# The 31 dependent steps of a block inverse issued on POOL in place of DVE

## The chip, the cores and the metric

The kernel runs on one core of a Trainium2 chip. The metric is the device time of one launch in microseconds (us), the median of several runs. One execution was also taken by the profiler; every row below comes from it. PE is the tensor engine, DVE the vector engine, ACT the scalar engine, POOL the GpSimd engine, and SP the engine whose queue issues the DMAs.

## The reference

Two transformer blocks run one after the other on one sequence of 1024 tokens of width 1024. The first has a projection, a sliding-window attention, an RWKV-7 time mix, an output projection and a convolution-gated feed-forward network. The second has gated linear attentions and a stick-breaking attention. Only the RWKV part is touched:

```python
def step(state, inp):
    r_t, w_t, k_t, v_t, kk_t, a_t = inp
    sa = jnp.einsum('bhvk,bhk->bhv', state, -kk_t)
    state = (state * w_t[:, :, None, :]
             + sa[..., None] * (kk_t * a_t)[:, :, None, :]
             + v_t[..., None] * k_t[:, :, None, :])
    return state, jnp.einsum('bhvk,bhk->bhv', state, r_t)
...
_, o = lax.scan(step, state0, (tmaj(rh), tmaj(heads(decay)), tmaj(kh), tmaj(vh), tmaj(kk), tmaj(heads(a))))
```

There are 8 heads of width 64. A token's state update depends on the state that the token before it left. The kernel takes the tokens in chunks of 64, and inside a chunk the dependence becomes the inverse of a triangular 64 x 64 matrix.

## The kernel before

The sequence is cut into two halves of 512 tokens, and each half into four pieces of 128 tokens. The RWKV part of one piece is numbered e (0 to 7) and has three stages. `rwkv_a(e)` makes the operands and the triangular matrices (tile `MT`); it uses POOL for two products of 128 x 512 (`kk`, `r`) and for one power (`rn`, line 127). `rwkv_b(e)` inverts the matrices. `rwkv_c(e)` runs over the two chunks of the piece with the state and normalises the result; its power on POOL is `rsd`.

In `rwkv_b` the 32 diagonal blocks of 32 x 32 of one piece go through DRAM (`l_d`) into the tile `Lq`, one block on each partition and four copies of all of them. The inverse `XT` is then built by forward substitution in 31 steps. A step is one product into `ot` (line 544) and one sum into `XT` (line 545), so there are 62 instructions a piece and 496 in all, each dependent on the one before it. Between steps the stage yields, and other work is written in between. The result goes by DMA to `x_d` (line 548) and from there into `TT` (line 550); DVE transposes `TT` into `XQ` (line 553), and PE takes `XQ` in the products of line 558 and goes on to the whole 64 x 64 inverse.

All products with weights are made of three passes, with high and low parts of both factors. The helper `split` (line 130) makes the parts: ACT copies to `wh`, and DVE subtracts to `wl`. Weights come in through tiles with three buffers (`wr`, `wh`, `wl`), loaded by line 137 from SP's queue.

The order of the work is made in two steps, both before anything runs. `weave` takes the stages of several streams in turn by the costs that they yield (0.7 for one step of the inverse) times a rate for each stream. A planner then gives each engine's queue and SP's queue one fixed order, by priorities, by what depends on what, and by when it takes a thing to be ready. `Stream` raises the priority of the RWKV stages by a number of places (`AA`, `AB`, `AC`). Nothing is reordered at run time: each queue is worked off in order, and an instruction whose input is late holds up all that stands behind it in its queue. The streams of the first four pieces are woven with the projection; those of the last four with the output projection and the feed-forward network:

```python
weave(Stream(proj_all(), RF), Stream(stage_a(), R1, AA), Stream(stage_b(), R2, AB), Stream(stage_c(), R3, AC), also=[attend])
...
def rest():
    for e in range(4, 8):
        yield from rwkv_a(e, 1)
        yield from rwkv_b(e, 1)
        yield from rwkv_c(e, 1)
```

Elementwise operations go through the helper `tt` (line 80), whose last argument is the engine. `V` is DVE and `G` is POOL. `PE0` and `PE1` (line 90) name the engines of even and odd steps, and both are `V`.

Of the kernel before, what the change touches and what calls it, by code (L numbers as in the profile page):

```python
# [65 lines left out]
def tile_hybrid_blocks(ctx: ExitStack, tc: tile.TileContext, a: dict, out: bass.AP):  # L66
    nc = tc.nc
    V, S, G, T, SY = nc.vector, nc.scalar, nc.gpsimd, nc.tensor, nc.sync
# [7 lines left out]
    def act(out, in_, func, **kw):  # L76
        S.activation(out=out, in_=in_, func=func, **kw)  # L77

    def tt(out, in0, in1, op, eng=None):
        (eng or V).tensor_tensor(out=out, in0=in0, in1=in1, op=op)  # L80
# [6 lines left out]
        (eng or V).tensor_scalar(out=out, in0=in0, scalar1=s1, scalar2=s2, op0=op0, **kw)  # L87

    DQ = SY
    PE0, PE1 = V, V  # L90
    ADD, SUB, MUL, MAX, MIN = ALU.add, ALU.subtract, ALU.mult, ALU.max, ALU.min

    cst = pool("cst", 1)
# [296 lines left out]
    def after(what):  # L390
        while what not in done1:
            yield None
# [7 lines left out]
    def flat(t):  # L400
        return t.rearrange("p a b -> p (a b)")
# [125 lines left out]
    def rwkv_b(e, dbl):  # L527
        yield from after(("a", e))
        z, AR, MT, UV, BKt, EC, bon, l_d, x_d = rws[e]
        psr_t = psb_r  # L530


        Lq = rw.tile([128, 32, 32], F32, tag="Lq" if dbl == 2 else "t4", name="Lq", bufs=1)
        for g in range(4):
            DQ.dma_start(out=Lq[32 * g:32 * g + 32], in_=l_d)
        XT = rw.tile([128, 8, 32], F32, name="XT")
        G.memset(XT, 0.0)
        for g in range(4):
            G.memset(flat(XT[32 * g:32 * g + 32])[:, g:256:36], 1.0)
        ot = rw.tile([128, 80], F32, name="ot")  # L540
        for s in range(31):
            n, m = s // 4 + 1, 31 - s
            o3 = ot[:, 0:n * m].rearrange("p (a b) -> p a b", a=n)
            tt(o3, Lq[:, s:s + 1, s + 1:32].to_broadcast([128, n, m]), XT[:, 0:n, s:s + 1].to_broadcast([128, n, m]), MUL, PE1 if s % 2 else PE0)
            tt(XT[:, 0:n, s + 1:32], XT[:, 0:n, s + 1:32], o3, ADD, PE1 if s % 2 else PE0)
            yield 0.7
        for g in range(4):
            DQ.dma_start(out=x_d.rearrange("q (a g) t -> g q a t", g=4)[g], in_=XT[32 * g:32 * g + 32])
        for b in range(2):
            DQ.dma_start(out=TT[32 * b:32 * b + 32, :, 32 * b:32 * b + 32], in_=x_d[16 * b:16 * b + 16].rearrange("q s t -> s q t"))  # L550

        XQ = rw.tile([64, 16, 32], F32, name="XQ")
        V.transpose(out=XQ[0:32], in_=TT[0:32, :, 0:32])
        qp = psr_t([128, 8, 32])
        for n in range(8):
            for b in range(2):
                q = 8 * b + n
                T.matmul(out=qp[32 + 64 * b:64 + 64 * b, n, :], lhsT=MT[0:32, q // 2, q % 2, 96:128], rhs=XQ[0:32, q, :],
                         start=True, stop=True)
        for b in range(2):  # L560
            act(XQ[32:64, 8 * b:8 * b + 8], qp[32 + 64 * b:64 + 64 * b], AF.Copy)
        yield 4
        qp = psr_t([128, 8, 32])
        for n in range(8):
            for b in range(2):
                q = 8 * b + n
                T.matmul(out=qp[64 * b:64 * b + 32, n, :], lhsT=XQ[32:64, q, :], rhs=TT[32:64, q, 32:64], start=True, stop=True)
        for b in range(2):
            act(TT[0:32, 8 * b:8 * b + 8, 32:64], qp[64 * b:64 * b + 32], AF.Copy)
        yield 3  # L570


        ap_ = psr_t([128, 8, 64])
        for q in range(16):
            hb = 64 * (q % 2)
            T.matmul(out=ap_[hb:hb + 64, q // 2, :], lhsT=UV[0:64, q // 2, hb:hb + 64], rhs=TT[:, q, :], start=True, stop=True)
        act(AR[:, :, 1, :], ap_, AF.Copy)
        yield 3

        wp_ = psr_t([128, 8, 64])  # L580
        for n in range(8):
            for b in range(2):
                q = 8 * b + n
                hb = 64 * (q % 2)
                T.matmul(out=wp_[64 * b:64 * b + 64, n, :], lhsT=MT[64:128, q // 2, q % 2, 64:128], rhs=UV[64:128, q // 2, hb:hb + 64],
                         start=True, stop=True)
        W0 = []
        for b in range(2):
            W0.append(rw.tile([64, 8, 64], F32, tag="W0" if dbl == 2 else "t3", name="W0", bufs=2))
            V.tensor_copy(W0[b], wp_[64 * b:64 * b + 64])  # L590
        yield 4
        yp = psr_t([128, 8, 64])
        for n in range(8):
            for b in range(2):
                T.matmul(out=yp[64 * b:64 * b + 64, n, :], lhsT=TT[:, 8 * b + n, :], rhs=W0[b][:, n, :], start=True, stop=True)
        for b in range(2):
            act(flat(UV[0:64, 4 * b:4 * b + 4, :]), flat(yp[64 * b:64 * b + 64]), AF.Copy)
        yield 4
        done1.add(("b", e))
# [224 lines left out]
    def stage_b():  # L824
        for e in range(4):
            yield from rwkv_b(e, 2)
# [12 lines left out]
# [5 lines that stand above are left out]
# [888 lines left out]
```

## Time and profile before

| what | value |
|---|---|
| median of 3 runs | 2511.98 us (2508.98 to 2515.89) |
| the profiled execution, its own time | 2509.05 us |
| span from its first to its last instruction | 2507.3 us |
| mean granted clock of PE over the span | 0.981 |

The profiled execution's own time is 1.75 us more than its span, and 2.9 us less than the median of the runs. A busy share is the time in which an engine had an instruction in work. The granted clock is the share of PE's full speed (2.4 GHz) that the chip allowed; it has two levels, full and half, so a mean of 0.9 over a stretch is a fifth of it at half speed. In rows with an arrow and a releaser, the number in brackets is how long the engine had been idle, and behind `<-` stands what ended that.

### The profile page before, as it was taken

Reading aid. Unit: us, or ns where it says so; the run is one execution under the profiler, and the core shown is the slowest. Engines: PE = TensorE matmul, PEld = TensorE weight load, DVE = VectorE, ACT = ScalarE, POOL = GpSimd, SP = SyncE. Lnnn points to the kernel's source line nnn. Section 1 sums busy time; section 2 is a strip of 40 time slices with the busy share of each in tenths; the row PEclk is TensorE's granted clock in tenths of the full one; section 3 lists DMA queues with packets and bytes.
Section 4 is the critical chain, followed back from the end, with each engine's and each line's share of the span. In section 5 each row is a group of like instructions: output and inputs, shape, how many; then the busy total and the mean of one; then the engine's idle time right before and its main releaser. Section 6 shows DMA issues by size and latency. Waiting matters only on the chain.

```text
span 2507.3 us, 40921 instructions
## 1 busy us (share of the span) xinstructions
PE 2375.0 (95%) x15310; PEld 1863.7 (74%) x15310; DVE 1688.9 (67%) x3678; ACT 1171.0 (47%) x2223; POOL 100.2 (4%) x138
## 2 busy tenths in 40 slices
PE   6989998889999999999999999999999999999997
PEld 5767776767777777778778887788877667777665
DVE  5466556667686776663885555555568988788887
ACT  4345433654433434343543333343345575656863
POOL 1001000100000000000000000000000000000000
PEclk9999999979999999999999999999999999999989
DMA  6433323555352342333463332243256335342446
GB/s 203 147 116 89 99 87 94 160 162 159 97 172 79 107 140 91 92 124 96 161 205 94 97 93 93 81 156 100 94 166 223 99 112 179 105 132 91 144 136 244
DMA packets 219997, 320.77 MB, mean 128 GB/s; under 512 B 56956, under 2 KB 95508, under 8 KB 219799
## 3 DMA queue, kind: packets, MB, share of 16 engines
q1 hardware_dynamic: 219798, 318.17, 40.5%
q8 instruction: 120, 1.97, 0.3%
q14 instruction: 79, 0.64, 0.1%
HBM read 270.88 MB, written 47.21 MB: 127 GB/s over the span
## 4 chain that ended last, share of the span: by engine, by line
PE 60%; DVE 9%; DMA 3%; issue 3%; ACT 2%; POOL 1%; SPq 0%; POOLq 0%; ACTq 0%; DVEq 0%
PE g L153 32%; PE d L153 12%; DVE wl L80 1%; PE s L1416 1%; PE R L1520 1%; PE gr L773 1%; DVE cv L83 1%; PE gr L774 1%; PE gr L775 1%; PE x L773 1%; PE x L775 1%; PE x L774 1%; DVE tmp L80 1%; PE z L1505 1%; PE po L1538 1%
## 5 line engine op out<-in xcount | busy, mean ns | idle before, releaser
L77 ACT ACTIVATE wh<-wr 128x512 fp32r<-128x512 f32 x712 | 442.8, 626 | 639.8 <-PE g L153 216.9
L153 PE MATMUL g<-hi,wl 128*128 128x512 f32 (+1 forms) x1680 | 677.1, 403 | 13.5 <-DVE lo L80 4.1
L153 PE MATMUL g<-hi,wh 128*128 128x512 f32 (+1 forms) x1680 | 667.2, 397 | 0.0
L153 PE MATMUL g<-lo,wh 128*128 128x512 f32 (+1 forms) x1680 | 665.5, 396 | 0.0
L80 DVE TENSOR_TENSOR wl<-wr,wh 128x512 fp32r<-128x512 f32 x712 | 484.7, 685 | 207.2 <-ACT wh L77 205.9
L153 PEld LDWEIGHTS g<-hi,wl 128*128 128x128 f32 (+1 forms) x1680 | 317.1, 189 | 91.0 <-issue 8.6
L153 PEld LDWEIGHTS g<-hi,wh 128*128 128x128 f32 (+1 forms) x1680 | 316.7, 188 | 71.7 <-issue 2.6
L153 PEld LDWEIGHTS g<-lo,wh 128*128 128x128 f32 (+1 forms) x1680 | 317.2, 189 | 68.5 <-issue 3.7
L83 DVE SCALAR_TENSOR_TENSOR cv<-g,CW,cv 128x511 f32<-128x511 f32 (+1 forms) x256 | 190.8, 745 | 179.3 <-ACT cv L77 179.0
L153 PE MATMUL d<-hh,wl 128*128 128x512 f32 x512 | 202.5, 399 | 12.7 <-ACT hh L77 7.5
L153 PE MATMUL d<-hl,wh 128*128 128x512 f32 x512 | 202.1, 395 | 0.1
L153 PE MATMUL d<-hh,wh 128*128 128x512 f32 x512 | 200.8, 392 | 0.0
L77 ACT ACTIVATE cv<-g,CW 128x512 f32<-128x512 f32 x128 | 99.5, 777 | 181.5 <-PE g L153 181.1
L80 DVE TENSOR_TENSOR acc<-d,acc 128x512 f32<-128x512 f32 x112 | 76.4, 689 | 94.7 <-PE d L153 94.6
L153 PEld LDWEIGHTS d<-hh,wl 128*128 128x128 f32 x512 | 95.8, 189 | 41.8 <-ACT hh L77 12.0
L153 PEld LDWEIGHTS d<-hl,wh 128*128 128x128 f32 x512 | 96.5, 188 | 23.0 <-DVE hl L80 3.6
L153 PEld LDWEIGHTS d<-hh,wh 128*128 128x128 f32 x512 | 96.6, 189 | 20.3 <-issue 0.2
L773 PE MATMUL gr<-wl,hi 128*128 128x512 f32 x200 | 83.4, 418 | 7.3 <-DVE wl L80 6.6
L774 PE MATMUL gr<-wh,lo 128*128 128x512 f32 x200 | 80.1, 400 | 0.0
L775 PE MATMUL gr<-wh,hi 128*128 128x512 f32 x200 | 79.7, 399 | 0.0
L127 POOL TENSOR_TENSOR rs<-ms,half_c 128x1 f32<-128x1 f32 x48 | 29.4, 612 | 1085.1 <-DVE ms L87 1077.2
L77 ACT ACTIVATE hh<-cv 128x512 fp32r<-128x512 f32 x64 | 40.4, 631 | 65.5 <-DVE cv L80 65.4
(508 smaller groups left out, 3475.7 us busy)
## 6 DMA issues: line engine op xcount, KB each, us to landing
wr<-in_w_up_dram SPq DMA_DIRECT2D x256, 256.0 KB, 2.7
wr<-in_w_in_dram SPq DMA_DIRECT2D x160, 256.0 KB, 2.9
wr<-in_w_down_dram SPq DMA_DIRECT2D x128, 256.0 KB, 2.6
wr<-in_w_out_dram SPq DMA_DIRECT2D x100, 256.0 KB, 3.0
wr<-in_w_values_dram SPq DMA_DIRECT2D x64, 256.0 KB, 2.9
wa<-in_w_ada_dram SPq DMA_DIRECT2D x24, 512.0 KB, 4.3
xt<-x SPq DMA_DIRECT2D x24, 512.0 KB, 4.5
xt<-in_x_dram SPq DMA_DIRECT2D x16, 512.0 KB, 3.6
```

The source lines that it names most:

```text
L77: S.activation(out=out, in_=in_, func=func, **kw)
L80: (eng or V).tensor_tensor(out=out, in0=in0, in1=in1, op=op)
L83: V.scalar_tensor_tensor(out=out, in0=in0, scalar=scalar, in1=in1, op0=op0, op1=op1)
L127: G.tensor_tensor(out=dst, in0=src, in1=half_c[0:src.shape[0], 0:src.shape[1]], op=ALU.pow)
L153: T.matmul(out=ps, lhsT=l, rhs=r, start=(first and n == 0), stop=(last and n == 3 * len(wk) - 1))
L773: T.matmul(out=p, lhsT=hi[:, k, tok], rhs=wl, start=first, stop=False)
L774: T.matmul(out=p, lhsT=lo[:, k, tok], rhs=wh, start=False, stop=False)
L775: T.matmul(out=p, lhsT=hi[:, k, tok], rhs=wh, start=False, stop=last)
L1416: T.matmul(out=ps[hb:hb + 64, l - 2, :], lhsT=xl(hb, l, 0, 64), rhs=xl(hb, l, 0, 64), start=True, stop=True)
L1505: T.matmul(out=z[:, h, :], lhsT=Ks[:, p, h, kb * 128:(kb + 1) * 128], rhs=q[:, h, off:], start=q is ql, stop=q is qh)
L1520: T.matmul(out=R[:, :, c0:c1], lhsT=m, rhs=x[:, :, c0 - off:c1 - off], start=start and x is sl, stop=x is sh, skip_group_check=not start)
L1538: T.matmul(out=po[hb:hb + 64, c0:c1], lhsT=Vh[:, kb, hd * 64:(hd + 1) * 64], rhs=ar[:, h, c0 - off:c1 - off], start=(kb == top), stop=(kb ...
```

## The change

Both instructions of each of the 31 steps are issued on POOL. The names `PE0` and `PE1` are dropped. Nothing else in the text of the kernel differs; the two fills of `XT` (lines 537 and 539) were on POOL already.

```diff
     DQ = SY
-    PE0, PE1 = V, V
     ADD, SUB, MUL, MAX, MIN = ALU.add, ALU.subtract, ALU.mult, ALU.max, ALU.min
...
         for s in range(31):
             n, m = s // 4 + 1, 31 - s
             o3 = ot[:, 0:n * m].rearrange("p (a b) -> p a b", a=n)
-            tt(o3, Lq[:, s:s + 1, s + 1:32].to_broadcast([128, n, m]), XT[:, 0:n, s:s + 1].to_broadcast([128, n, m]), MUL, PE1 if s % 2 else PE0)
-            tt(XT[:, 0:n, s + 1:32], XT[:, 0:n, s + 1:32], o3, ADD, PE1 if s % 2 else PE0)
+            tt(o3, Lq[:, s:s + 1, s + 1:32].to_broadcast([128, n, m]), XT[:, 0:n, s:s + 1].to_broadcast([128, n, m]), MUL, G)
+            tt(XT[:, 0:n, s + 1:32], XT[:, 0:n, s + 1:32], o3, ADD, G)
             yield 0.7
```

## Rows read from the trace of the kernel before

**Rows 1.** The page: engines, busy us (share of the span), instructions.

```profile
PE 2375.0 (95%) x15310; PEld 1863.7 (74%) x15310; DVE 1688.9 (67%) x3678; ACT 1171.0 (47%) x2223; POOL 100.2 (4%) x138
```

**Rows 2.** Windows cut at each chain's first and last step: busy us, granted clock.

```profile
core 0: us, PE busy (x) PEld busy (x) DVE busy (x) ACT busy (x) POOL busy (x), PEclk, DMA share, GB/s
157.00:186.70 29.70, 25.14 (x127) 18.97 (x126) 26.25 (x105) 12.22 (x24) 0.00 (x0) 0.90 0.47 150
...
307.30:340.20 32.90, 29.47 (x152) 23.16 (x153) 27.00 (x108) 15.79 (x41) 2.68 (x2) 0.90 0.18 57
...
516.60:554.90 38.30, 32.16 (x156) 25.32 (x155) 31.10 (x109) 21.65 (x49) 2.06 (x3) 0.82 0.46 143
...
1011.30:1040.70 29.40, 27.58 (x112) 21.63 (x111) 25.93 (x90) 9.95 (x16) 0.00 (x0) 0.94 0.27 81
sum 258.40, PE 235.04 PEld 184.11 DVE 226.34 ACT 100.40 POOL 9.57; mean PE 29.38 PEld 23.01 DVE 28.29 ACT 12.55 POOL 1.20
```

**Rows 3.** Sum over windows of the seven stretches between the chains, same columns.

```profile
sum 625.00, PE 597.59 PEld 474.12 DVE 374.32 ACT 282.02 POOL 38.47; mean PE 85.37 PEld 67.73 DVE 53.47 ACT 40.29 POOL 5.50
```

**Rows 4.** Waits of PE, 100 to 1060 us: for what, us, times, longest.

```profile
PE trx L247 <- DVE y L83: 6.3, 2, 5.9
```

**Rows 5.** The tile ot: duration ns min/median/max, first and last start us.

```profile
L80 DVE TENSOR_TENSOR ot<-Lq,XT x248: 164/211/727, 157.0 to 1040.3; 128x60 f32<-128x60 f32 x12, 128x54 f32<-128x54 f32 x8, 128x66 f32<-128x66 f32 x8, 128x28 f32<-128x28 f32 x8
```

**Rows 6.** POOL's groups by form: busy us, mean ns, idle before.

```profile
L127 POOL TENSOR_TENSOR rs<-ms,half_c 128x1 f32<-128x1 f32 x48 | 29.4, 612 | 1085.1 <-DVE ms L87 1077.2 <-DVE XT L80 7.9
L127 POOL TENSOR_TENSOR rn<-n,half_c 128x8 f32<-128x8 f32 x8 | 14.7, 1840 | 43.2 <-DVE n L87 43.2
...
L80 POOL TENSOR_TENSOR kk<-k,P 128x512 f32<-128x512 f32 x8 | 8.4, 1046 | 85.6 <-DMA k<-rkv_d 75.5 <-PE ra L495 10.1
...
L539 POOL MEMSET XT<- 32x8 f32 x32 | 3.4, 105 | 1.8
```

**Rows 7.** Timeline of POOL, then of DVE, 225 to 236 us: start, us.

```profile
227.46 1.05 POOL L80 TENSOR_TENSOR kk<-k,P 128x512 f32<-128x512 f32 x1
234.37 1.55 POOL L80 TENSOR_TENSOR r<-r,P 128x512 f32<-128x512 f32 x1 [5.86 <-DVE AR L80]
...
227.54 1.52 DVE L80 TENSOR_TENSOR og<-og,rsd 128x512 f32<-128x512 f32 x1 [1.82 <-POOL rsd L127]
...
234.34 0.68 DVE L80 TENSOR_TENSOR o<-o,bon 128x512 f32<-128x512 f32 x1
```

**Rows 8.** DVE's groups in the windows 379.9 to 401.7 and 699.8 to 736.8.

```profile
L80 DVE TENSOR_TENSOR wl<-wr,wh 128x512 fp32r<-128x512 f32 x6 | 4.1, 685 | 0.0
...
L80 DVE TENSOR_TENSOR wl<-wr,wh 128x512 fp32r<-128x512 f32 x12 | 8.2, 686 | 0.5 <-ACT wh L77 0.5
L83 DVE SCALAR_TENSOR_TENSOR adam<-wa,sc,adam 128x1024 f32<-128x1024 f32 x5 | 6.4, 1281 | 0.5 <-DMA wa<-in_w_ada_dram 0.5
```

**Rows 9.** The chain of piece 3 in the timelines of SP, DVE and PE.

```profile
369.65 2.49 SPq L535 DMA_DIRECT2D Lq<-l_d  x4
379.88 0.18 DVE L80 TENSOR_TENSOR ot<-Lq,XT 128x31 f32<-128x31 f32 x1
401.76 2.53 SPq L548 DMA_DIRECT2D x_d<-XT  x4
404.40 1.47 SPq L137 DMA_DIRECT2D wr<-in_w_out_dram  x2
406.08 0.87 SPq L550 DMA_DIRECT2D TT<-x_d  x2
409.38 0.70 DVE L553 STREAM_TRANSPOSE XQ<-TT 32x512 f32<-32x512 f32 x1 [0.53 <-DMA TT<-x_d]
410.13 0.69 PE L558 MATMUL rb__3723<-XQ,MT 32*32 32x32 f32 x32 [0.41 <-DVE XQ L553]
```

**Rows 10.** Waits of DVE over the span: for what, us, times, longest.

```profile
DVE sgw L462 <- POOL rn L127: 12.6, 8, 1.8
DVE XQ L553 <- DMA TT<-x_d: 1.3, 3, 0.5
```

## The prediction

> **What bounds the kernel now.** I read the page first. PE is busy for 95% of the span, and POOL for 4% [rows 1]. So the change takes work from the second busiest engine and gives it to an idle one, and it can help only where PE stands because of DVE. The windows tell how much that is. Cut at the first and the last step of each of the eight chains, they hold 258.4 us, in which PE is busy for 235.0 and DVE for 226.3 [rows 2]: DVE is 88% busy there and PE idle for 23.4 us (9.1%). The seven stretches between the chains hold 625.0 us, with DVE busy for 374.3 (60%) and PE idle for 27.4 us (4.4%) [rows 3]. PE stands about twice as much while a chain runs. The granted clock is also below 1 in four of the eight chain stretches (0.90, 0.90, 0.82, 0.94) [rows 2]; by their lengths that is 0.10 x 29.7 + 0.10 x 32.9 + 0.18 x 38.3 + 0.06 x 29.4 = 14.9 us of PE's full speed. Not all of it belongs to the chain: in the stretch with 0.82, PE stands once for 5.9 us for `y`, which is the normalisation after the output projection [rows 4].
>
> Then I followed one chain through the queues. For piece 3, SP issues the loads of `Lq` until about 372, the first step starts on DVE at 379.88, the last step ends at 401.7, `x_d` is issued at 401.76, `TT` at 406.08, DVE turns it into `XQ` at 409.38 after 0.53 us of waiting for it, and PE takes that at 410.13 after 0.41 us of waiting [rows 9]. The reader is to see how tight these places are. Over all eight pieces DVE stood for `TT` only three times, 1.3 us in all [rows 10]: the fixed order has the users of the chain just where the chain ends.
>
> **What goes from DVE.** 496 instructions of 0.211 us median [rows 5] are 105 us of busy time, 13 us a chain. Off the path this is worth nothing; on it, what counts is PE's idle time. If the chain stretches came down to the idle share of the others, 0.044 x 258.4 = 11.3 us would be left of 23.4, a gain of 12.1; with all the lost clock back it would be 27.0. The lower end is 0, as DVE still has its other work in one file. I take 10: most of the 12.1, hardly any of the clock, since its largest part hangs on `y` [rows 4].
>
> **What a step costs on POOL.** The trace has no small product or sum there. A step works on 31 to 80 elements a partition, on the mean 50.3 (the sum of n x m over the 31 steps is 1560). POOL's product of 512 elements takes 1.046 us and its fill of 8 elements 0.105 us [rows 6]. With the fill's time as the fixed part, the product is 0.105 + 1.84 ns an element, so an instruction takes 0.105 + 0.093 = 0.20 us, and 62 of them 12.3 us. The upper end comes from the powers: 0.612 us for one element and 1.840 for eight make 0.44 us fixed [rows 6]; the product then has 1.18 ns an element, an instruction takes 0.50 us, and 62 take 31 us. I take 0.33, a little nearer the product and the fill, which have no power in them: 20.5 us a chain.
>
> **What the two engines do to each other.** At 227.46 POOL begins `kk`, 1.05 us; at 227.54 DVE begins `og<-og,rsd`, and it takes 1.52 us instead of the 0.69 of its passes of that size; at 234.37 POOL's `r`, just behind the start of DVE's `o<-o,bon`, takes 1.55 instead of 1.05 [rows 6 to 8]. Each waits until the other's pass is over. The Trainium skill, SBUF — State Buffer, section "Who interferes with whom", has this as a rule: a DVE instruction with two SBUF inputs and a GpSimd instruction that reads SBUF exclude each other for the whole instruction; the trace agrees (1.52 against 0.69). By that rule the weight splits count and the passes that read PSUM do not. So DVE's passes with two SBUF inputs lie on top of the chain: in one chain stretch the splits alone are 4.1 us, in another the splits and `adam` are 8.2 + 6.4 = 14.6 [rows 8]. A chain of 20.5 us in place of a stretch of 258.4 / 8 = 32.3 us meets 0.63 of that, 2.6 to 9.3 us, in the middle 6. The chain is then about 26 us; it can start when `Lq` has landed, which is before DVE took it up [rows 9], so by the clock it should end no later than now.
>
> **Where that puts the stall.** The end by the clock is not what decides, but the end against the places in the order, which is made anew before the run. Three queues are in file behind the chain: SP at `x_d`, with weight loads behind it; DVE at `XQ`, with the next splits behind it; PE at line 558, with the next products behind it [rows 9]. The trace shows how the order treats POOL: the user of the power `rn` stands right behind it each time, and DVE stood for it 8 times of 8, 12.6 us in all [rows 10], 1.6 of the 1.84 us that the power takes [rows 6]. So the order has had POOL's results too early, by nearly their whole time. If it has the steps at their bare time and nothing for the mutual waits, `x_d`, `XQ` and line 558 come some 6 us too early a chain. While DVE stands, POOL works undisturbed, so I take a third off: 4 us of PE's time a chain. PE at 95% cannot make it up: 8 x 4 = 32 us. Below, this is 0, when the order has room; above, 62 x (0.50 - 0.33) = 10.5 us come on top of 6, 16 a chain, 130 us in all. The fills, the DMAs and their number do not change. The powers and products of the neighbouring pieces now share POOL with the steps; I cost them at nothing beyond this, as no more than three of them fall into the four stretches shown [rows 2].
>
> **The sum.** 2509.05 - 10 + 32 = 2531 us, for an execution like the profiled one, which is 2.9 us under the median of the runs.
>
> **The rivals.**
> - *The chain fits its places, and DVE's relief is what is left.* This is the other side. For it: POOL is free for 96% of the span [rows 1], and `Lq` is there some 4 us before DVE starts on it: the last load is issued about 8 us ahead, and a transfer with its issue takes about 4, as from `x_d` to `TT` [rows 9]. Against it: `rn`. The time is 2509 - 10 = 2499, down to 2490 if part of the clock comes back. It decides when a chain is less than 10 / 8 = 1.25 us late against its places.
> - *Nothing to measure.* Relief and stalls cancel, or PE stood for other things all along: 2509, within 0.3%. That bound, 7.5 us, is about what a measurement of this kernel can tell from no change. For it: only 23.4 of 2507 us are in play. It needs a chain late by 0.3 to 2.2 us.
> - *POOL is slow at small work.* With 0.50 us a step, the chain is 31 + 6 us, longer than DVE's 32.3, and 12 us late a chain after a fourth is taken off: 2509 - 10 + 96 = 2595. For it: the powers' fixed 0.44 us. Against it: the fill of 0.105 [rows 6]. The Trainium skill, GPSIMD Engine Reference, section 3.1, gives about 2.6 cycles an element at 1.2 GHz for two inputs and calls DVE about twice as fast; an estimate from that page is 50.3 x 2.6 / 1.2 = 109 ns of elements a step. The rows give 59 to 93 ns, and what a step costs beside them the page leaves open.
>
> **How the numbers follow.** The forecast has a chance of 0.43, slow small steps 0.07, the fitting chain 0.28, nothing to measure 0.22. So: slower 0.50, same 0.22, faster 0.28. The likeliest is slower, 2531; its own range is 2520 to 2572, from 2.6 to 9 us late a chain. The range over all cases is 2494 to 2572: it leaves out the best part of the fitting chain below, and slow steps above, together about 0.17.
>
> **What the profile after would show.** Steps right: 496 instructions of about 0.33 us on POOL, start to start, longer where DVE's two-input passes lie; DVE's busy time down by about 105 us; DVE's `XQ` and PE's line 558 waiting for `TT` in most pieces, about 4 us each, and SP standing at `x_d`. Wrong: if `XQ` still waits for no more than 1.3 us in all, the order had room, and the time is at or below that of before. The prediction would also be wrong if the new order moves the work of other pieces, so that the gaps of PE come from something that the chain doesn't touch.

## The result, and the profile after

The changed kernel takes 2636.32 us (median; 2623.52 to 2641.21), against 2510.48 us (2506.85 to 2515.89) for the kernel before on the same chip: a ratio of 1.0498, 95% interval 1.0472 to 1.0523. It is slower, as forecast, but by 126 us and not by 22, and outside the stated range of 2494 to 2572. The profiled execution has a span of 2632.7 us and a mean granted clock of 0.946. Lines of the changed kernel carry numbers one lower than before: `XQ` is line 552 and PE's product 557.

The page's line of engines (busy us, share, instructions):

```profile
PE 2437.0 (93%) x15310; PEld 1909.4 (73%) x15310; DVE 1615.4 (61%) x3182; ACT 1171.1 (44%) x2223; POOL 274.0 (10%) x634
```

Against [rows 1], PE's busy time is up by 62.0 us with the same 15310 matmuls, and its idle time (span less busy) went from 132.3 to 195.7 us, up by 63.4. The sum, 125.4, is the whole difference of the two spans. So half of the loss is PE standing, and half is PE doing the same work slower. The granted clock fits that: a mean of 0.946 over 2632.7 us is 2 x 0.054 x 2632.7 = 284 us at the lower level of 1.2 GHz, against 95 us for 0.981 over 2507.3.

Next the windows cut at each chain's first and last step, first, second and last chain and the sum (columns as in [rows 2]), and the sum over the seven stretches between them:

```profile
151.00:178.10 27.10, 20.44 (x96) 15.53 (x96) 12.63 (x21) 9.52 (x18) 22.31 (x63) 0.89 0.25 79
224.10:254.70 30.60, 20.36 (x94) 15.43 (x94) 17.87 (x43) 9.63 (x20) 25.98 (x65) 0.83 0.22 65
...
1122.10:1147.80 25.70, 21.12 (x89) 16.14 (x87) 13.64 (x24) 8.11 (x14) 20.89 (x62) 1.00 0.14 41
sum 219.70, PE 172.28 PEld 129.96 DVE 109.70 ACT 67.13 POOL 181.69; mean PE 21.53 PEld 16.25 DVE 13.71 ACT 8.39 POOL 22.71
```

```profile
178.10:224.10 46.00, 38.81 (x395) 32.27 (x396) 16.10 (x47) 14.57 (x44) 3.34 (x7) 0.62 0.29 78
...
339.00:384.50 45.50, 39.57 (x292) 28.45 (x291) 9.68 (x18) 10.22 (x25) 0.79 (x7) 0.55 0.30 85
...
sum 777.10, PE 715.03 PEld 567.69 DVE 414.29 ACT 313.78 POOL 40.14; mean PE 102.15 PEld 81.10 DVE 59.18 ACT 44.83 POOL 5.73
```

The chains are shorter than before (219.7 us against 258.4), and DVE is half idle in them (109.7 of 219.7). But PE stands for 47.4 us in them instead of 23.4, and for 62.1 between them instead of 27.4 [rows 2, 3]. The granted clock of 0.62 and 0.55 lies in the stretches behind the first and the third chain.

The steps themselves, by the tile `ot`:

```profile
L80 POOL TENSOR_TENSOR ot<-Lq,XT x248: 208/296/1102, 151.0 to 1147.3; 128x60 f32<-128x60 f32 x12, 128x54 f32<-128x54 f32 x8, 128x66 f32<-128x66 f32 x8, 128x28 f32<-128x28 f32 x8
```

A stretch of POOL's and of DVE's timeline in the chain of piece 1 (start, us, idle before):

```profile
238.51 0.30 POOL L80 TENSOR_TENSOR ot<-Lq,XT 128x64 f32<-128x64 f32 x1
238.89 0.32 POOL L80 TENSOR_TENSOR XT<-XT,ot 128x64 f32<-128x64 f32 x1
...
241.90 1.64 POOL L126 TENSOR_TENSOR rn<-n,half_c 128x8 f32<-128x8 f32 x1
...
247.00 0.81 POOL L80 TENSOR_TENSOR ot<-Lq,XT 128x48 f32<-128x48 f32 x1
247.89 0.29 POOL L80 TENSOR_TENSOR XT<-XT,ot 128x48 f32<-128x48 f32 x1
...
254.51 0.21 POOL L80 TENSOR_TENSOR XT<-XT,ot 128x8 f32<-128x8 f32 x1
```

```profile
234.51 0.17 DVE L87 TENSOR_SCALAR n<-ra 128x8 f32<-128x8 f32 x1 [0.33 <-PE ra L456]
...
243.58 0.52 DVE L461 COPY sgw<-rn 128x512 f32<-128x512 f32 x1 [8.56 <-POOL rn L126]
...
246.99 0.69 DVE L80 TENSOR_TENSOR kk<-kk,ia 128x512 f32<-128x512 f32 x1
```

An instruction of a step with 64 elements takes 0.30 to 0.32 us, and the next starts 0.38 us after it (238.51 to 238.89). At 247.00 a product of 48 elements takes 0.81 us: DVE's `kk<-kk,ia`, with two SBUF inputs, has begun 0.01 us earlier and ends at 247.68, and the product ends at 247.81; the sum of the same size behind it takes 0.29. Between 235 and 243.5, where DVE stands, the steps run undisturbed. DVE made `n` at 234.68; POOL takes up `rn` only at 241.90, as it stands behind steps, and DVE waits for it for 8.56 us with its splits behind it.

One place in full, piece 7, in the timelines of SP, DVE and PE (compare [rows 9]):

```profile
1116.27 2.76 SPq L534 DMA_DIRECT2D Lq<-l_d  x4
1119.12 4.21 SPq L136 DMA_DIRECT2D wr<-in_w_up_dram  x3
1125.64 5.34 SPq L136 DMA_DIRECT2D wr<-in_w_down_dram  x3
1147.80 2.52 SPq L547 DMA_DIRECT2D x_d<-XT  x4
```

```profile
1141.25 0.79 DVE L80 TENSOR_TENSOR wl<-wr,wh 128x512 fp32r<-128x512 f32 x1
1154.75 0.70 DVE L552 STREAM_TRANSPOSE XQ<-TT 32x512 f32<-32x512 f32 x1 [12.71 <-DMA TT<-x_d]
1155.39 0.64 DVE L80 TENSOR_TENSOR hl<-cv,hh 128x512 fp32r<-128x512 f32 x1
```

```profile
1156.08 0.80 PE L152 MATMUL d<-hl,wh 128*128 128x512 f32 x1 [12.32 <-DVE hl L80]
```

SP has `x_d` six loads behind `Lq`, and stands from about 1131 to 1147.80 with the further loads behind it. DVE stands for 12.71 us at `XQ`; the split `hl` is behind it, and PE waits 12.32 us for that. PE's own line 557 comes only at 1163.20: what stalls PE is what is queued behind the chain's user on DVE.

In pieces 4 to 6 it is what stands behind `x_d` in SP's queue. In piece 6 the store `ada_d` is issued after `x_d`, DVE stands for it, and PE stands 10.9 us for the sum `acc` behind that; in piece 4 a weight load comes after `x_d`, ACT and DVE stand for it, and PE 12.9 us behind them. The first line is DVE's, the second ACT's:

```profile
987.68 0.75 DVE L87 TENSOR_SCALAR adam<-wa,sc 128x1024 f32<-128x1024 f32 x1 [13.45 <-DMA ada_d<-adam]
548.22 0.63 ACT L77 ACTIVATE wh<-wr 128x512 fp32r<-128x512 f32 x1 [15.05 <-DMA wr<-in_w_out_dram]
```

DVE's and PE's waits over the span (for what, us, times, longest):

```profile
DVE XQ L552 <- DMA TT<-x_d: 38.5, 6, 12.7
DVE sgw L461 <- POOL rn L126: 26.3, 8, 8.6
```

```profile
PE d L152 <- DVE acc L80: 19.8, 8, 10.9
PE ra L464 <- DVE sgw L461: 19.0, 5, 8.0
PE gr L772 <- DVE wl L80: 18.5, 6, 12.9
PE d L152 <- DVE hl L80: 12.3, 1, 12.3
PE rb__1503 L557 <- DVE XQ L552: 12.0, 1, 12.0
...
PE rb__3101 L557 <- DVE XQ L552: 5.9, 1, 5.9
```

The two waits of [rows 10] went from 1.3 to 38.5 and from 12.6 to 26.3 us. PE's long stalls are 6 to 13 us each, under five different names, as different work stands behind `XQ`, `x_d` or `sgw` in each piece. Those behind a chain's users are 12.0, 5.9, 12.9, 7.0, 10.9 and 12.3 us (pieces 0, 2, 4, 5, 6 and 7), 61 us in all; two more, of 8.0 and 7.9 us, are for `sgw`.

### The profile page after: what moved, and what is told of

Same layout as the page of the kernel before. It is cut to its first block, busy times and chain, and to the rows that moved or that the text cites. A ratio compares the mean times of both kernels' runs of the same rounds, so it can differ in the third digit from the quotient of the medians.

```text
span 2632.7 us, 40937 instructions
## 1 busy us (share of the span) xinstructions
PE 2437.0 (93%) x15310; PEld 1909.4 (73%) x15310; DVE 1615.4 (61%) x3182; ACT 1171.1 (44%) x2223; POOL 274.0 (10%) x634
## 3 DMA queue, kind: packets, MB, share of 16 engines
q1 hardware_dynamic: 219798, 318.17, 38.5%
## 4 chain that ended last, share of the span: by engine, by line
PE 67%; POOL 9%; DVE 8%; issue 6%; DMA 5%; ACT 3%; SPq 1%; POOLq 0%; DVEq 0%; ACTq 0%
PE g L152 34%; PE d L152 11%; POOL XT L80 3%; POOL ot L80 3%; PE gr L772 1%; PE gr L773 1%; DVE wl L80 1%; PE gr L774 1%; PE s L1415 1%; PE R L1519 1%; PE a_ps L727 1%; PE x L772 1%; PE trx L246 1%; PE x L774 1%; PE x L773 1%
## 5 line engine op out<-in xcount | busy, mean ns | idle before, releaser
L152 PE MATMUL d<-hl,wh 128*128 128x512 f32 x512 | 205.9, 402 | 12.4 <-DVE hl L80 12.3
L126 POOL TENSOR_TENSOR rs<-ms,half_c 128x1 f32<-128x1 f32 x48 | 29.6, 617 | 1086.2 <-DVE ms L87 1086.2
L80 POOL TENSOR_TENSOR ot<-Lq,XT 128x60 f32<-128x60 f32 (+24 forms) x248 | 86.5, 349 | 206.6 <-DMA Lq<-l_d 188.0
L80 POOL TENSOR_TENSOR XT<-XT,ot 128x60 f32<-128x60 f32 (+24 forms) x248 | 86.9, 351 | 19.2
```

Of the source, the lines that this page charges most:

```text
L126: G.tensor_tensor(out=dst, in0=src, in1=half_c[0:src.shape[0], 0:src.shape[1]], op=ALU.pow)
L152: T.matmul(out=ps, lhsT=l, rhs=r, start=(first and n == 0), stop=(last and n == 3 * len(wk) - 1))
```

## The experiments

Theory A: the fixed order puts the users of the chain too early. Theory B: mutual exclusion of POOL's steps and DVE's passes is the loss itself. Theory C: it is the powers and products that stand behind the steps in POOL's file. Ratios are against the kernel before on the same chip. In every run the order is made anew, so that it can differ in more than the edit.

**e1_room.** The steps stay on POOL; `x_d` is put behind about as many weight loads as before the change.

```diff
+    loads = []
...
-        SY.dma_start(out=wr, in_=src)
+        loads.append(SY.dma_start(out=wr, in_=src))
...
-        for g in range(4):
-            DQ.dma_start(out=x_d..., in_=XT[32 * g:32 * g + 32])
+        place = [45,55,66,79,117,167,213,256][e]
+        while len(loads) <= place:
+            yield 1
+        with tc.issue_after(loads[place].ins):
+            for g in range(4):
+                DQ.dma_start(out=x_d..., in_=XT[32 * g:32 * g + 32])
```

> The steps stay on POOL; only the place of the transfer to x_d in SP's fixed order is moved, behind the same number of weight loads that stood before it when the steps were on DVE (46, 56, 67, 80, 118, 168, 214 and 259 for the eight pieces, against 44, 48, 55, 63, 94, 160, 206 and 251 in the changed kernel). What uses the chain's result then moves back with it. Theory A, the order has the users of the chain too early because it takes the chain to be some 12 us shorter than it is: the waits of DVE for TT fall from 38 us to under 8, and the time is 2495 to 2530. Theory B, POOL and DVE slow each other through their shared access to SBUF: the same instructions meet each other, so the time stays above 2600. Theory C, the powers of the neighbouring pieces stand in POOL's file behind the steps: DVE's wait for rn stays at some 26 us, and the time is 2540 to 2600.

2552.68 us, ratio 1.0163 (1.0139 to 1.0187): 84 of the 126 us are gone with the same instructions on the same engines, so B is not the main loss. The time is above A's range (2495 to 2530) and in C's, but DVE's wait for `rn` fell from 26.3 to 14.1 us, where C had it stay. DVE's wait at `XQ` for `TT` fell from 38.5 to 3.6 us. The new order moved the loads of `Lq` too, so that the places did not fit everywhere: in piece 1 `x_d` came 50 us after the chain's end, while in pieces 6 and 7 PE still stood 9.9 and 11.0 us for `XQ` (in piece 6 DVE had stood 14.7 us for a load behind `x_d` in SP's queue). PE's longest stall, 12.9 us for `y`, is in part C: DVE stood 4.8 us for the power `rs`, which POOL took up only after the last steps of piece 4.

**e2_cut** and **e3_cut_dve.** The four transfers to `x_d` and the two to `TT` are left out, so that nothing waits for the chain's end (the inverse's 32 x 32 blocks stay zero); steps on POOL in the first, on DVE in the second.

```diff
-        for g in range(4):
-            DQ.dma_start(out=x_d..., in_=XT[32 * g:32 * g + 32])
-        for b in range(2):
-            DQ.dma_start(out=TT..., in_=x_d...)
```

> Leaves out the transfers of the steps' result to x_d and TT, so the products behind them work on zeros; all 496 steps still run on POOL and nothing waits for them. Theory A: no user, no stall, 2490 to 2515, within 10 us of the same cut with the steps on DVE. Theory B: the steps still lie beside DVE's passes, at least 2560. Theory C: the powers still stand behind steps, 2520 to 2560.

> The kernel before, on DVE, with the same transfers left out (products behind them on zeros): the other half of the comparison. All theories: a little under the kernel before, 2495 to 2511, since DVE stood for TT for only 1.3 us there.

2523.76 us, ratio 1.0050 (1.0032 to 1.0068), and 2504.47, ratio 0.9978 (0.9960 to 0.9997). The first is above A's range and just in C's. Of the 126 us, all but 19 hang on somebody waiting for the chain. The 19 are visible in PE's waits of e2_cut:

```profile
PE ra L464 <- DVE sgw L461: 15.2, 6, 10.0
...
PE ra L657 <- DVE og L80: 9.7, 4, 4.8
```

`sgw` and `og` are the users of POOL's `rn` and `rsd`. DVE stood for `rn` for up to 11.3 us in one piece, and PE for 10.0 us behind it; in e3_cut_dve the longest wait for `rn` is 1.8 us. So what is left without a user of the chain shows up as powers that come late behind its steps.

**e4_half.** Steps 0 to 15 on DVE, 16 to 30 on POOL.

```diff
-..., MUL, G)
-..., ADD, G)
+..., MUL, G if s >= 16 else V)
+..., ADD, G if s >= 16 else V)
```

> Steps 0 to 15 on DVE, 16 to 30 on POOL: 30 of 62 instructions a piece move. Theory A: the chain is late by the moved half, some 6 us a piece, so the loss of 125 us shrinks to 40 to 70, a time of 2550 to 2580. Theory B: 2560 to 2580 as well, as half of the meetings are left; it is told apart by the waits for TT, which A has at 12 to 20 us in all and B at under 5.

2593.41 us, ratio 1.0337 (1.0305 to 1.0369): a miss for both theories. Half of the steps on POOL cost two thirds of the loss; why so much stays open. DVE's waits for `TT` were 25.5 us, more than A's 12 to 20 and far from B's 5. PE stood at `XQ` five times, for 4.1 to 10.6 us; the wait for `rn` was as before (1.8 at most). Of the 80.6 us by which its span of 2587.9 is longer, 35.6 are PE idle and 45.0 the same work slower (PE busy 2420.0).

**e5_first** and **e6_rest.** POOL has the steps of pieces 0 to 3 only, or of 4 to 7 only (`G if dbl == 2 else V`, and `dbl == 1`).

> Only pieces 0 to 3 have their steps on POOL; pieces 4 to 7 have them on DVE. In the changed kernel the first half's last product of the mix was ready at 454.8 us against 440.7, so if the loss is local to the chains (each late chain costs what PE stands for it and the half clock behind it), this kernel loses about 14 us, up to 30 with the half clock behind piece 3: 2525 to 2540. The rival, that each late chain costs the same wherever it lies, gives half of 126: 2573.

> Only pieces 4 to 7 have their steps on POOL. If the loss is local, this kernel has the other 95 to 112 us: 2605 to 2622. The rival of equal shares gives 2573. If the two halves' losses do not add up to 126, the order made anew is part of the loss.

2577.13 us, ratio 1.0265 (1.0230 to 1.0300), and 2552.93, ratio 1.0173 (1.0157 to 1.0189): 68 and 44 us, together 112 of the 126. My shares were wrong: I had read a milestone of the first half (14 us later), and that moves with the order. Equal shares (2573) are 4 us off in the first and 20 in the second. In e6_rest PE stands once where each of the four chains is taken up: 10.5, 6.9, 10.7 and 11.9 us. In e5_first the stalls are of like length (11.4, 8.0, 7.9, 6.5 and 3.5 us). By span and busy time, PE's idle time is up by 30 us in both (2552.6 - 2390.1 and 2577.6 - 2415.7, against 132.3); the same work takes 15 us more in e6_rest and 41 in e5_first. So the two halves differ in how much slower the work is and not in the standing; the mean granted clocks are 0.970 and 0.961.

**e7_room2.** e1_room with places nearer to where its chains ended: `[45,51,63,77,117,171,219,262]`.

> As e1_room, but the places of the x_d transfer are nearer to where its chains ended by the clock: 7, 7, 8, 10, 17, 15, 10 and 5 weight loads lie between the last load of Lq and x_d, where e1_room had 7, 11, 8, 8, 15, 11, 8 and 6. If the place decides, SP no longer stands 5 and 15 us at x_d in pieces 5 and 6, and piece 1 is no longer taken up 50 us after its end: 2520 to 2545, under e1_room's 2553. The last piece has less room still, so its wait of about 5 us stays. If most of what e1_room still loses is mutual exclusion or POOL's file, the time stays at 2545 to 2560.

2528.49 us, ratio 1.0078 (1.0061 to 1.0095): 107 of 126 us are back by eight numbers that say where `x_d` stands. PE's two largest stalls between 100 and 1240 us are 4.9 and 6.5 us, both in the last two pieces, where the places were still early.

**e8_fills** and **e11_fills_kept.** Of each chain only the first step is left; the other 60 instructions are fills on POOL of 256 elements a partition, which read nothing (the inverse's blocks are zero). e8_fills has the transfers left out as in e2_cut, e11_fills_kept has them.

```diff
-            tt(o3, Lq..., XT..., MUL, G)
-            tt(XT..., XT..., o3, ADD, G)
+            if s:
+                G.memset(XT, 0.0)
+                G.memset(XT, 0.0)
+            else:
+                tt(o3, Lq..., XT..., MUL, G)
+                tt(XT..., XT..., o3, ADD, G)
```

> As e2_cut (the transfers out of the chain are left out and nothing waits for its end; the inverse's blocks are zero), but of each chain only the first step is left; the other 60 instructions are fills of 256 elements a partition, which read nothing and take about as long as a step. If mutual exclusion with DVE's passes made e2_cut's 19 us over the same cut with the steps on DVE, this kernel loses it: 2505 to 2510. If the 19 us come from the powers rn and rsd and the products of neighbouring pieces that stand behind the steps in POOL's file, they stay: 2518 to 2530.

> The changed kernel with x_d and TT kept, but of each chain only the first step is left, and the other 60 instructions are fills of XT, 256 elements a partition (so the inverse's blocks are zero). In e8_fills a fill took 0.31 us and 0.37 from start to start, so a chain is about 23 us, against 25.5 to 31.6 with the steps. The order made for it has 9 weight loads between Lq and x_d in the last three pieces, where the changed kernel has 6 and the one before 14. If the stall comes from the length that the order gives the steps, and not from POOL's queue as such, most of it goes: about 2 us late a chain instead of 8 to 12, 2510 to 2540. If a chain on POOL is late in any case, it stays over 2590.

e8_fills: 2508.34 us, ratio 0.9994 (0.9978 to 1.0011). POOL is nearly as busy (256.7 us) and the powers stand among the fills, but no wait for `rn` is longer than 2.0 us. So standing in POOL's file need not make the powers late. The time is in the range given for mutual exclusion, but whether the 15 us against e2_cut are exclusion or the order's count of a step, this run doesn't separate: the order is made for fills here.

e11_fills_kept bears most on the main question: 2500.52 us (2489.29 to 2510.91), ratio 0.9951 (0.9927 to 0.9974), 10 us under the lower of its two ranges. A chain of 62 instructions on POOL, with `x_d`, `XQ` and PE waiting for its end, need not be late: DVE's waits for `TT` are 5.4 us in all and PE's for `XQ` 0.9. SP's queue in piece 7:

```profile
999.70 0.88 SPq L534 DMA_DIRECT2D Lq<-l_d  x2
1000.67 5.27 SPq L136 DMA_DIRECT2D wr<-in_w_up_dram  x3
1008.24 10.54 SPq L136 DMA_DIRECT2D wr<-in_w_down_dram  x5
...
1024.46 0.33 SPq L136 DMA_DIRECT2D wr<-in_w_down_dram  x1
1025.99 2.53 SPq L551 DMA_DIRECT2D x_d<-XT  x4
```

The order gave the fills 9 loads between `Lq` and `x_d`, and SP had issued the last of them 1.2 us before `x_d`. It gave the steps 6, though a chain of steps is longer (25.7 us in piece 7, against about 23 of fills). The fills also read nothing and are hardly stretched (0.32 us on the mean, 0.31 undisturbed), so this chain lacks the mutual waits; with the steps those are about 4 us a chain, less than the stalls of 6 to 13.

**e9_none** and **e10_control.** e3_cut_dve with only the first step left, so that neither engine has the others; and the kernel before, steps on DVE, with e1_room's list of places.

> The transfers out of the chain are left out as in e2_cut and e3_cut_dve, and of each chain only the first step is left, on DVE: neither DVE nor POOL has the other 480 instructions (the inverse's blocks are zero). This measures what it is worth to take them from DVE, apart from all that they cost elsewhere. The prediction took 10 us of gain (at least 0, at most 27), so against 2504.5 of e3_cut_dve: 2494. The rival, from e8_fills, which had DVE relieved as well and came out at 2508.3: the relief is worth nothing, 2500 to 2508.

> The kernel before, steps on DVE, with x_d put at a written place as in e1_room (same list of places). If the place is what moved e1_room and e7_room2, and the writing of it costs nothing, this stays near 2510: 2505 to 2525, with at most a few us for places that are later than the chain's end. If writing a place by hand harms the order by itself, it comes out at 2530 or more, and part of what e1_room and e7_room2 still lose is not POOL's.

e9_none: 2520.34 us (2502.69 to 2527.78), ratio 1.0023 (1.0004 to 1.0041). No gain from taking 480 instructions off DVE, where I had expected 10 us. Against e3_cut_dve it is 16 us slower by the medians and 11 by the ratios, with less to do on DVE and nothing added elsewhere. That leaves the new order as the likely reason, and then of the differences between runs only those well above 10 us are safe; the 19 us of e2_cut and the 15 of e8_fills are not. e10_control: 2511.81 us, ratio 0.9998 (0.9985 to 1.0011): writing the places by hand costs nothing here. So what e1_room and e7_room2 still lose belongs to POOL's steps and to their new orders, in shares that are not shown.

## Why the prediction was right in direction and wrong in size

**The step's price: right.** Forecast 0.33 us an instruction and 20.5 us a chain. Taking for each of the 62 places in a chain the second shortest of its eight durations, a bare chain is 17.4 us of instructions and 61 pauses of 0.078 us: 22.1 us, 0.36 an instruction. A step works on 8 to 76 elements, not "31 to 80"; the mean of 50.3 was right. From 8 to 76 elements (0.21 to 0.33 us) an element costs 1.8 ns. The Trainium skill, GPSIMD Engine Reference, section 3.1, has 2.6 cycles an element at 1.2 GHz, an estimate of 2.2 ns, a little more than measured. The fixed part, some 0.2 us and the pause, is the larger one here.

**Mutual exclusion: right, a little smaller.** The 62 instructions of a chain take 1.8 to 6.1 us more than the bare 17.4, on the mean 4.3, where 6 was taken (2.6 to 9.3). The Trainium skill, SBUF — State Buffer, section "Who interferes with whom", gives the rule; at 247.00 the trace agrees, 0.81 us against 0.27 to 0.29 for undisturbed ones of that size.

**The chain's length: right.** 25.5 to 31.6 us, on the mean 27.5 (219.7 / 8), where 26 was forecast, and all but that of piece 3 (25.5 against 21.8) are shorter than before. From the issue of `Lq` to that of `x_d` it took 29.6 to 49.3 us, against 32.1 to 47.9 before: less in six pieces, and 1 us more in pieces 1 and 2. So by the clock most chains would have ended in time.

**Where that puts the stall: the place right, the size wrong.** This is the step that failed. The prediction took it that the order has "the steps at their bare time and nothing for the mutual waits", so that a chain would be late by the waits alone, 6 us, less a third: 4 us of PE a chain, 32 in all. PE stood for the chains' users 61 us in all, nearly twice that, in six stalls of 6 to 13 us. In piece 7 PE stood 12.3 us; a chain of 25.7 us that ends 12.3 us late had 13.4 us in the order, 0.22 us an instruction (an estimate, from those two rows), far below the bare 0.36. The loads give nearly the same: 6, where fills of about 23 us got 9, are 15 us (an estimate too). So the order had the steps at well under their bare time. That is inferred, as no run shows the order's own figure. The runs bear it out: with more room for `x_d`, and the same steps on POOL, 84 and 107 of 126 us come back, and fills, to which the order gave 9 loads and not 6, are on time. The warning was in [rows 10]: the order had made DVE wait 1.6 of the 1.84 us that `rn` takes. I read that as "too early, by nearly their whole time" and then let the order know the bare time of the steps all the same. If a row shows that the order doesn't know POOL's durations, the bound on the lateness is the whole chain. The upper end of the term as written, 16 us a chain and 130 us, was about what came, but by luck: I let it hang on slow steps only, which didn't come, and left it out of the range.

**Costed at nothing, and not nothing: the clock.** The prediction counted PE's standing and no slower work after it. Of the 125.4 us, 62.0 are slower work. The granted clock is low behind a stall (0.62 and 0.55 in two stretches behind chains).

**Costed at nothing, and partly not: the powers behind the steps.** Late `rn` stalled DVE for 26.3 us instead of 12.6, and PE for 8.0 us at a time. It seems to be the same cause: in e7_room2, with the steps on POOL, no wait for `rn` is longer than 1.8 us, and among fills none is longer than 2.0 (e8_fills). The other power, `rsd`, is still late in e7_room2, by up to 7.0 us.

**The relief of DVE: not settled.** Of the 5.9 us for `y` that the prediction put into the stretch with 0.82, 2.2 lie behind it (PE stood from 551.2 to 557.1, and the stretch ends at 554.9). DVE's busy time fell by 73.5 us and not by 105, since 211 ns is an instruction's duration and neighbours overlap (e9_none against e3_cut_dve: 71.5 us for 480 instructions, 0.149 each). Forecast gain: 10 us. e11_fills_kept is 12 to 13 us faster than the kernel before, but e8_fills and e9_none are 4 and 16 us slower than e3_cut_dve, which has all steps on DVE (medians, on different chips). Each has an order made anew, and that scatters by as much as the gain; what the relief alone is worth stays open.

Of the rivals, the fitting chain has its case in e11_fills_kept, where the order gives a chain of fills its length; that it came out near 2499 us is partly luck, as the relief isn't settled. The 2595 us rival was nearer to the size than the forecast, with the wrong cause: an instruction takes 0.36 us and not 0.50. No version with the real steps on POOL beat the kernel before; the best is e7_room2, 0.8% slower.

## What to carry to other kernels

In a kernel whose queues are put in a fixed order beforehand, moving a dependent chain to another engine changes two things: how long it takes, and how long the order believes it takes. Look for a row in which the order already misjudges that engine, and bound the lateness by the whole chain, for each queue in which a user of the chain stands with other work behind it. If the chain by itself is fast enough, try to give its users room before undoing the move, and count a stall of the matmul engine with the slower work that follows it. Each change makes the order anew, which alone seems to move the time by 10 us or more here, so small differences between such runs prove little.

## What was not expected of the hardware

How long the clock stays at its lower level differs much from stall to stall. Three windows of the changed kernel: behind the stall of 12.0 us in piece 0, from inside that of 5.9 us in piece 2, and behind that of 12.3 us in piece 7. The last line is the kernel before, at the same place in the work as the second:

```profile
175.60:213.10 37.50, 27.81 (x281) 23.20 (x282) 11.18 (x36) 8.85 (x28) 2.60 (x14) 0.50 0.32 88
342.90:383.90 41.00, 36.08 (x264) 25.85 (x265) 8.93 (x17) 7.33 (x16) 0.74 (x5) 0.50 0.28 80
...
1156.00:1197.00 41.00, 40.91 (x326) 32.22 (x326) 18.43 (x32) 12.73 (x23) 0.00 (x0) 0.93 0.23 72
340.20:379.90 39.70, 37.69 (x415) 29.89 (x414) 16.84 (x36) 11.62 (x21) 0.74 (x5) 1.00 0.36 100
```

In the second window the stall ends at about 347.8; from there on PE is busy in the profile without a pause (36.08 us in all), and the granted clock is 0.50, 1.2 GHz, to the window's end at 383.9: 36 us of work at half speed. A product of 64 x 64 takes 0.31 us there, against 0.22 in the kernel before. Behind the stall of piece 7, 0.93 over 41 us is some 6 us at half speed, and the rest at 2.4 GHz. The length of the stall alone doesn't decide it: in piece 0, behind one as long (it ends at 185.3), the clock is 0.50 to the window's end at 213.1, with PE busy. The work behind the stalls differs. In piece 0 the first 17 us hold no product of 128 x 512, only smaller ones of the RWKV mix and others; in the second window 25 of the 264 are of 128 x 512; in piece 7 all are, until at about 1161.8 one takes 0.40 us in place of 0.63. The small products of the second window don't lower the clock by themselves: the kernel before had them at 1.00, among more of 128 x 512 (last line). This fits e5_first, whose stalls cost more than those of e6_rest. That the kind of product behind a stall is the cause was not tried by itself.
